# The per-layer input gets a tile of its own, and its load moves up the load queue

## The chip, the cores and the metric

The kernel runs on one core of a Trainium2 chip. The metric is device time in microseconds (us) of one execution; lower is better. A core has five engines that run their own instruction streams in order and wait for one another through semaphores: TensorE (PE: matrix products, weight loads beside them), VectorE (DVE), ScalarE (ACT), GpSimd (POOL) and SyncE (SP), which here issues nearly all loads from memory.

## The reference

One layer of a decoder trunk on 256 tokens of width 1024, in float32. Three token mixers run in parallel: sparse attention with an indexer that keeps the top 64 keys, dilated attention in which three groups of queries share keys and values, and block attention. Each adds a relative-position bias to its logits. Their gated sum goes through an output product and a layer norm, then through a feed-forward part and a second layer norm. The per-layer input p enters only near the end:

```
proj = x @ w_in                                  # queries, keys, values of the three mixers
gates = sigmoid(x @ w_gate)
merged = gates[0]*(o_a @ w_br_a) + gates[1]*(o_b @ w_br_b) + gates[2]*(o_c @ w_br_c)
x = layer_norm(ALPHA*x + merged @ w_out, ln1_g, ln1_b)
h = square(relu(x @ w_up)) @ w_down
ple = sigmoid(x @ w_ple_gate) * (p[i] @ w_ple)   # p: the per-layer input, 256 tokens x 256
x = layer_norm(ALPHA*x + h + ple, ln2_g, ln2_b)
```

## The kernel before

All products run as three products of "split" operands: a float32 tile becomes a high part, rounded to the format of the products (ScalarE's cast), and a low part, the difference (VectorE's subtraction, for some weights shared with GpSimd). A weight goes through such a split on the way in: SyncE loads 512 KB or less into one of five `raw` buffers (L71), ScalarE casts it to `whi` (L75), VectorE and GpSimd write `wlo` (L79), TensorE multiplies (L136). A load can go out once the split of an earlier weight has freed its buffer.

The order on each engine is set by the program's scheduler, from the order of the code and the data each instruction needs; `issue_after(ins)` adds the rule that what is written inside stands behind `ins` on that engine.

The stretch that matters lies between the dilated attention and the block attention:

- The dilated attention treats two pairs of heads, j = 0 and 1. For each, `toeplitz` loads two bias tiles T (three loads each, from a table in memory, L188), `slots` computes the logits and the softmax in two large buffers with the tag `eb` (pool `wk2`, two buffers), and `attend` transposes the result (L314), casts and splits it into `pt` (L321, L322), multiplies it with the values V (L324, L325) and drains the product: ScalarE copies one half to `ov` (L328), VectorE adds the halves twice (L329 to `ov`, L330 to `o`). `pair_out` splits `o` into `op` (L333, L334).
- Then the per-layer input, transposed on the host, is loaded into `pr` (L471), cast to `ph` (L472) and split to `pl` (L473). `ph` and `pl` are kept; they are multiplied only after the first layer norm. The tile `pr` takes one of the two `eb` buffers.
- Then the values of the block attention are computed (weights `wvb`), and for j = 0, 1, 2 a key tile (`k_pair`, L228 and L229), a query tile (`q_pair`, L217 and L218) and their logits (`logits`, L274). In between stand products for the gates, `fill("g")`, whose result ScalarE turns into G (L241).

```
pr = wk2.tile([128, 2, S], F32, name="pr", tag="eb")     # L470
nc.sync.dma_start(pr, pT)
act.copy(ph, pr)
dve.tensor_tensor(pl, pr, ph.bitcast(F32), op=ALU.subtract)
values(u_vb, 384, 5, 6, False)
```

Of the kernel before, what the change touches and what calls it, by code (L numbers as in the profile page):

```python
# [11 lines left out]
F32 = mybir.dt.float32  # L12
F32R = mybir.dt.float32r
ALU = mybir.AluOpType
# [6 lines left out]
S = 256  # L21
# [10 lines left out]
N_U = 384  # L32
# [63 lines left out]
def hybrid_layer(ctx: ExitStack, tc: tile.TileContext, x0, xn, pT, wqk, wva, wvb, wg, wbc, wba,  # L96
                 wout, wup, wdq, wdn, wpg, wple, lnrow, rel, mask, out):
    nc = tc.nc
    pe, act, dve, pool = nc.tensor, nc.scalar, nc.vector, nc.gpsimd
# [22 lines left out]
    ph = keep.tile([128, 2, S], F32R, name="ph")  # L122
    pl = keep.tile([128, 2, S], F32R, name="pl")
# [5 lines left out]
    t = banks.tile([128, 512], F32, name="b4", tag="b4")  # L129
# [23 lines left out]
    pm = mid.enter_context(tc.tile_pool(name="pm", bufs=1))  # L153
# [9 lines left out]
    def add(*a):  # L163
        i = n_u[0]
        n_u[0] += 1
        return W.add(*a, by=DV if i < 58 else "v")
# [6 lines left out]
    for t in TASKS:  # L173
# [8 lines left out]
        else:  # L182
            u_q.append([add(wqk[int(t) - FIRST], 1024)])

    def toeplitz(h0, step):
        t = tp.tile([128, 3, 256], F32, name="T", tag="T")
        for i in range(3):
            nc.sync.dma_start(t[:, i], bass.AP(  # L188
                tensor=tabd.tensor,
                offset=tabd.offset + (h0 + i * step) * COPIES * N_U + 127,  # L190
                ap=[[N_U - 16, 8], [N_U - 1, 16], [1, 256]]))
        return t


# [39 lines left out]
    def fill(what):  # L234


        for w in what:
            if w == "g":
                ps = mmbank(256)
                gemm(ps, u_g[n_g[0]], xs)  # L240
                act.activation(G[:, n_g[0]], ps, AF.Tanh, scale=0.5)  # L241
                n_g[0] += 1
                continue
            f = n_c[0]
            n_c[0] += 1
            hi, lo = W.get(u_bc[f][0])
            ps = mmbank(512).rearrange("p (i s) -> p i s", i=2)
            for i, (k0, k1) in enumerate(((3, 5), (5, 8))):
                for k in range(k0, k1):
                    c = slice((k - 3) * 128, (k - 2) * 128)  # L250
                    prod(ps[:, i], (hi[:, c], lo[:, c]), (op[:, k, 0], op[:, k, 1]), k == k0,
                         k == k1 - 1)
            g = G[:, 3 * f + 1:3 * f + 3]
            dve.scalar_tensor_tensor(g, g, 1.0, ps, op0=ALU.add, op1=ALU.mult)
            dve.tensor_tensor(g[:, 0], g[:, 0], g[:, 1], op=ALU.add)
# [26 lines left out]
    op = pm.tile([128, 8, 2, S], F32R, name="op")  # L282

    def values(units, n, h0, heads, withiw):
        pss = [mmbank(512) for _ in range(2)]
        for i in range(4):
            hi, lo = W.get(units[i])
            for j in range(2):
                k = 2 * i + j
                c = slice(j * n, (j + 1) * n)  # L290
                for b in range(2):
                    t = slice(b * 128, (b + 1) * 128)
                    prod(pss[b][:, :n], (xh[:, k, t], xl[:, k, t]), (hi[:, c], lo[:, c]),
                         k == 0, k == KT - 1)
        v_out(pss, n, h0, heads, withiw)
# [7 lines left out]
            dve.tensor_tensor(V[:, b, h0:h0 + heads, DH:128], src,  # L303
                              V[:, b, h0:h0 + heads, 0:DH].bitcast(F32), op=ALU.subtract)

    n_pt = [0]

    def attend(heads, o):

        ts = []  # L310
        for i, (P, vh, h) in enumerate(heads):
            t = next(ps_t)
            for c in (1, 2, 0):
                m = pe.transpose(t[:, 128 * c:128 * c + 128], P[:, 128 * c:128 * c + 128], ident)  # L314
                if i or c != 1:
                    tc.keep_in_program_order(m)
            ts.append(t)
        for t, (P, vh, h) in zip(ts, heads):
            pt = pts[n_pt[0] % 2]
            n_pt[0] += 1  # L320
            act.copy(pt[:, 0], t[:, 0:384])  # L321
            dve.tensor_tensor(pt[:, 1], t[:, 0:384], pt[:, 0].bitcast(F32), op=ALU.subtract)  # L322
            v = next(ps_t).rearrange("p (a s) -> p a s", a=2)
            pe.matmul(v, lhsT=V[:, 0, vh], rhs=pt[:, :, 0:256], start=True, stop=False)  # L324
            pe.matmul(v[:, :, 128:256], lhsT=V[:, 1, vh], rhs=pt[:, :, 256:384], start=False,  # L325
                      stop=True)
            x = wk2.tile([64, 2, S], F32, name="ov", tag="ov")
            act.copy(x, v[64:128])  # L328
            dve.tensor_tensor(x, v[0:64], x, op=ALU.add)  # L329
            dve.tensor_tensor(o[64 * h:64 * h + 64], x[:, 0], x[:, 1], op=ALU.add)  # L330
# [26 lines left out]
    def slots(qs, k, Ts, vh, o):  # L357

        es = [wk2.tile([128, 3, 384], F32, name="eb", tag="eb") for _ in range(2)]
        mxs = [sm.tile([128, 2, 3], F32, name="mxb", tag="mxb") for _ in range(2)]  # L360
        for g in range(3):
            s = logits(qs[g], k)
            for h in range(2):
                for b, t in enumerate((Ts[h][:, g, 128:256], Ts[h][:, g, :])):
                    dve.tensor_tensor_reduce(es[h][:, g, QC[b]], s[h][:, QC[b]], t, op0=ALU.add,
                                             op1=ALU.min, scale=1.0, scalar=-GONE,
                                             accum_out=mxs[h][:, b, g:g + 1])
        for h in range(2):
            e = es[h]
            m = sm.tile([128, 2], F32, name="mx", tag="mx")  # L370
            den = sm.tile([128, 2], F32, name="den", tag="den")
            dve.tensor_reduce(m, mxs[h], axis=AX.X, op=ALU.min)
            for b in range(2):
                act.activation(e[:, :, QC[b]], e[:, :, QC[b]], AF.Exp, bias=m[:, b:b + 1],
                               scale=-1.0, accum_out=den[:, b:b + 1])
            pool.tensor_tensor(e[:, 0], e[:, 0], e[:, 1], op=ALU.add)
            added[0] = pool.tensor_tensor(e[:, 0], e[:, 0], e[:, 2], op=ALU.add).ins
            scale_rows(e[:, 0], den)
        attend([(es[h][:, 0], vh + h, h) for h in (1, 0)], o)
# [36 lines left out]
    tp, wk, wk2, sm = (right(n, b) for n, b in (("tp", 3), ("wk", 3), ("wk2", 2), ("sm", 6)))  # L416
# [39 lines left out]
    for j in range(2):  # L456
        ps = feat(5 + 4 * j)
        k = k_pair(ps)
        fill("g")
        qs = []  # L460
        for g in range(3):
            qs.append(q_pair(feat(6 + 4 * j + g)))
            if g:
                fill("g")
        o = opair()
        Ts = [toeplitz(6 + 2 * j + h, 4) for h in range(2)]
        slots(qs, k, Ts, 1 + 2 * j, o)
        pair_out(o, 3 + j)
        fill("g")
    pr = wk2.tile([128, 2, S], F32, name="pr", tag="eb")  # L470
    nc.sync.dma_start(pr, pT)  # L471
    act.copy(ph, pr)  # L472
    dve.tensor_tensor(pl, pr, ph.bitcast(F32), op=ALU.subtract)  # L473
    values(u_vb, 384, 5, 6, False)
    fill("g")
    for j in range(3):
        ps = feat(13 + 2 * j)
        k = k_pair(ps)
        q = q_pair(feat(14 + 2 * j))
        s = logits(q, k)  # L480
        o = opair()
        for h in range(2):
            n = 2 * j + h
            if n % 3 == 0:
                T = toeplitz(18 + n, 1)
            e = head(s, T[:, n % 3, 128:256], T[:, n % 3], h)
            heads = [(e, 5 + n, h)] + (heads if h else [])
            if h:
                attend(heads, o)
            fill("g")  # L490
        pair_out(o, 5 + j)
# [4 lines left out]
    for j in range(3):  # L496
        q = q_pair(feat(19 + j))
        s = logits(q, kA)
        o = opair()
        for h in range(2):  # L500
            n = 2 * j + h
            if n % 3 == 0:
                T = toeplitz(n, 1)
            ta = wk.tile([128, 384], F32, name="ta", tag="ta")
            with tc.issue_after(W.pool):
                pool.tensor_tensor(ta[:, 0:128], T[:, n % 3, 128:256], am[:, 0:128], op=ALU.add)
                pool.tensor_tensor(ta[:, 128:384], T[:, n % 3], am[:, 128:384], op=ALU.add)
            e = head(s, ta[:, 0:128], ta[:, 128:384], h)
            heads = [(e, 0, h)] + (heads if h else [])
            if h:  # L510
                attend(heads, o)
            fill("gg" if n == 0 else "gc")
        done = pair_out(o, j)
# [153 lines left out]
    for b in range(2):  # L667
        t = slice(b * 128, (b + 1) * 128)
# [133 lines left out]
    for x in order:  # L802
# [4 lines left out]
        else:  # L807
            i = x - NP + 2
# [167 lines left out]
```

## Time and profile before

| | |
|---|---|
| median of 3 runs | 438.52 us (438.4 to 439.96) |
| the profiled execution | 436.83 us, of which the span is 435.0 us |
| TensorE busy | 424.3 us, 98% of the span |
| VectorE, ScalarE, GpSimd busy | 355.3, 274.7, 107.5 us |
| granted TensorE clock, mean | 0.996 |
| the chain that ended last | TensorE 92%, DMA 2%, VectorE 2%, ScalarE 1% |

The span runs from the first to the last instruction in the trace; the execution's own time is 1.83 us longer. A row of a timeline reads: start, length, engine, line of the kernel, operation, what is written from what, shape, count, and in brackets the idle time of the engine just before it with what ended that. A row of waits reads: who waited for whom, us in total, times, longest. Products are pipelined, so the lengths of neighbouring TensorE rows overlap; their starts tell the pace.

### The profile page before, as it was taken

What the parts mean: (1) busy time and instruction counts of PE and PEld (TensorE: products, weight loads), DVE (VectorE), ACT (ScalarE), POOL (GpSimd) and SP (SyncE); (2) the same over time, 40 slices, a digit from 0 to 9 for tenths busy, and PEclk for the clock granted to TensorE, in tenths of its full rate; (3) what the DMA queues carried; (4) which work ended last, traced back from release to release, by engine and by line L of the source; (5) the groups of instructions that cost most, each with busy time, mean ns of one, the idle gap of its engine ahead of it and who ended that gap; (6) DMA issues with size and microseconds to landing.
All of it is one profiled execution on the core that took longest, in us unless ns stands there. A gap on an engine that the chain in (4) does not pass through costs nothing.

```text
span 435.0 us, 7673 instructions
## 1 busy us (share of the span) xinstructions
PE 424.3 (98%) x2799; PEld 385.1 (89%) x2799; DVE 355.3 (82%) x625; ACT 274.7 (63%) x490; POOL 107.5 (25%) x98
## 2 busy tenths in 40 slices
PE   8999999999999999999999999999999999999993
PEld 8999999998999999999887888888888888888882
DVE  4978977577666588869988779999988898998984
ACT  6775375585777777746625567778887855665500
POOL 2564355392634656700000000000100000000001
PEclk9999999999999999999999999999999999999998
DMA  8897765465555334474980865656895378758411
GB/s 290 300 330 226 237 182 184 157 201 192 185 166 169 128 112 152 145 199 161 358 335 0 313 219 190 190 182 196 270 281 187 104 202 280 196 195 282 149 42 57
DMA packets 27690, 86.39 MB, mean 199 GB/s; under 512 B 2884, under 2 KB 6892, under 8 KB 27268
## 3 DMA queue, kind: packets, MB, share of 16 engines
q1 hardware_dynamic: 25872, 79.54, 55.5%
q0 software_dynamic: 640, 2.17, 2.8%
q10 hardware_dynamic: 1140, 4.19, 2.7%
q8 instruction: 22, 0.36, 0.3%
q14 instruction: 16, 0.13, 0.1%
HBM read 83.99 MB, written 1.90 MB: 197 GB/s over the span
## 4 chain that ended last, share of the span: by engine, by line
PE 92%; DMA 2%; issue 2%; DVE 2%; ACT 1%; POOLq 0%; POOL 0%; SPq 0%; DVEq 0%
PE mm L136 40%; PE b L136 23%; PE mm L705 14%; PE mm L707 7%; PE b L274 3%; PE b L413 2%; DMA G<-in_x_dram 1%; PE b L314 1%; DMA pr<-in_pT_dram 1%; PE b L324 1%; PE b L325 0%; DVE o L330 0%; DVE ov L329 0%; POOLq L972 0%; POOL rs L630 0%
## 5 line engine op out<-in xcount | busy, mean ns | idle before, releaser
L79 DVE TENSOR_TENSOR wlo<-raw,whi 128x1024 fp32r<-128x1024 f32 (+5 forms) x146 | 158.4, 1096 | 37.3 <-ACT whi L75 32.7
L75 ACT CAST whi<-raw 128x1024 fp32r<-128x1024 f32 (+3 forms) x146 | 146.1, 1011 | 46.6 <-PE b L136 11.7
L79 POOL TENSOR_TENSOR wlo<-raw,whi 128x384 fp32r<-128x384 f32 (+3 forms) x58 | 79.0, 1369 | 81.4 <-ACT whi L75 72.3
L136 PE MATMUL mm<-xl,whi 128*128 128x256 f32 x336 | 95.6, 284 | 0.0
L136 PE MATMUL mm<-xh,whi 128*128 128x256 f32 x336 | 95.0, 283 | 0.0
L136 PE MATMUL mm<-xh,wlo 128*128 128x256 f32 x336 | 94.7, 282 | 0.0
L136 PEld LDWEIGHTS mm<-xl,whi 128*128 128x128 f32 x336 | 63.3, 188 | 1.5
L705 PE MATMUL mm<-x,whi 128*128 128x512 f32 x256 | 64.1, 392 | 0.0
L136 PEld LDWEIGHTS mm<-xh,whi 128*128 128x128 f32 x336 | 63.3, 188 | 0.6
L136 PEld LDWEIGHTS mm<-xh,wlo 128*128 128x128 f32 x336 | 63.3, 188 | 0.3
L705 PEld LDWEIGHTS mm<-x,whi 128*128 128x128 f32 x256 | 46.1, 189 | 8.3
L136 PE MATMUL b<-whi,hT 128*128 128x512 f32 (+2 forms) x164 | 51.8, 381 | 0.0
L707 PEld LDWEIGHTS mm<-x,wlo 128*128 128x128 f32 x256 | 34.9, 190 | 2.5
L753 POOL DMA_DIRECT2D rows<-in_wdq_dram x4 | 3.6, 908 | 135.0 <-DVE wlo L79 81.7
L707 PE MATMUL mm<-x,wlo 128*128 128x256 f32 x256 | 35.7, 282 | 0.0
L136 PEld LDWEIGHTS b<-whi,hT 128*128 128x128 f32 x164 | 30.5, 188 | 5.8
L136 PE MATMUL b<-wlo,hT 128*128 128x512 f32 (+2 forms) x82 | 31.2, 381 | 0.0
L630 POOL TENSOR_TENSOR rs<-rs,half 128x1 f32<-128x1 f32 x4 | 4.1, 1032 | 101.5 <-DVE rs L629 101.5
L710 DVE TENSOR_REDUCE r<-mm 128x256 f32<-128x512 f32 x32 | 22.0, 688 | 5.2 <-PE mm L707 5.2
L241 ACT ACTIVATE G<-mm 128x256 f32<-128x256 f32 x24 | 9.1, 381 | 23.0 <-PE mm L136 22.9
L136 PE MATMUL mm<-op,whi 128*128 128x256 f32 x128 | 23.6, 281 | 0.0
L136 PE MATMUL b<-whi,x 128*128 128x512 f32 x64 | 20.4, 395 | 0.3 <-ACT x L658 0.3
(162 smaller groups left out, 736.6 us busy)
## 6 DMA issues: line engine op xcount, KB each, us to landing
raw<-in_wup_dram SPq DMA_DIRECT2D x32, 512.0 KB
raw<-in_wg_dram SPq DMA_DIRECT2D x24, 512.0 KB
raw<-in_wqk_dram SPq DMA_DIRECT2D x18, 512.0 KB
raw<-in_wdn_dram SPq DMA_DIRECT2D x16, 512.0 KB
raw<-in_wdq_dram SPq DMA_DIRECT2D x12, 512.0 KB
raw<-in_wout_dram SPq DMA_DIRECT2D x8, 512.0 KB
raw<-in_wpg_dram SPq DMA_DIRECT2D x8, 512.0 KB
T<-tabd SPq DMA_DIRECT2D x24, 128.0 KB
```

Of the source, the lines that this page charges most:

```text
L75: nc.scalar.copy(hi, r)
L79: low = e.tensor_tensor(lo[:, c], r[:, c], hi[:, c].bitcast(F32), op=ALU.subtract)
L136: m = pe.matmul(ps, lhsT=a[x], rhs=b[y], start=first and i == 0, stop=last and i == 2)
L241: act.activation(G[:, n_g[0]], ps, AF.Tanh, scale=0.5)
L274: m = pe.matmul(ss[h][:, QC[b]], lhsT=q[d, x, c], rhs=k[d, y, 0:128 * (b + 1)], start=i == 0, stop=i == 2)
L314: m = pe.transpose(t[:, 128 * c:128 * c + 128], P[:, 128 * c:128 * c + 128], ident)
L324: pe.matmul(v, lhsT=V[:, 0, vh], rhs=pt[:, :, 0:256], start=True, stop=False)
L413: pe.matmul(first[f], lhsT=w[:, k, 128 * f:128 * f + 128], rhs=x[:, k], start=k == i == 0, stop=k == KT - 1 and i == 2)
L630: pool.tensor_tensor(rs, rs, half, op=ALU.pow)
L705: pe.matmul(ps, lhsT=hi[:, cs[k]], rhs=x1[:, :, k], start=k == 0, stop=False)
L707: pe.matmul(ps[:, :, 0], lhsT=lo[:, cs[k]], rhs=x1[:, :, k, 0], start=False, stop=k == KT - 1)
L710: dve.tensor_reduce(r, ps.rearrange("p b a t -> p b t a"), axis=AX.X, op=ALU.add)
```

## The change

`pr` becomes a tile of 2 KB per partition in the pool `pm`, which holds what lives through the first half of the kernel. Its load stands behind the last load that `toeplitz` issued up to then, which is the third load of the second pair's second bias tile. Cast and split stand behind the last `pt` cast and the last `pt` split of the second pair.

```
     def toeplitz(h0, step):
         t = tp.tile([128, 3, 256], F32, name="T", tag="T")
         for i in range(3):
-            nc.sync.dma_start(t[:, i], bass.AP(
+            table[0] = nc.sync.dma_start(t[:, i], bass.AP(
...
-                ap=[[N_U - 16, 8], [N_U - 1, 16], [1, 256]]))
+                ap=[[N_U - 16, 8], [N_U - 1, 16], [1, 256]])).ins
...
-            act.copy(pt[:, 0], t[:, 0:384])
-            dve.tensor_tensor(pt[:, 1], t[:, 0:384], pt[:, 0].bitcast(F32), op=ALU.subtract)
+            cast[0] = act.copy(pt[:, 0], t[:, 0:384]).ins
+            cast[1] = dve.tensor_tensor(pt[:, 1], t[:, 0:384], pt[:, 0].bitcast(F32),
+                                        op=ALU.subtract).ins
...
-    pr = wk2.tile([128, 2, S], F32, name="pr", tag="eb")
-    nc.sync.dma_start(pr, pT)
-    act.copy(ph, pr)
-    dve.tensor_tensor(pl, pr, ph.bitcast(F32), op=ALU.subtract)
+    pr = pm.tile([128, 2, S], F32, name="pr")
+    with tc.issue_after(table[0]):
+        nc.sync.dma_start(pr, pT)
+    with tc.issue_after(cast[0]), tc.issue_after(cast[1]):
+        act.copy(ph, pr)
+        dve.tensor_tensor(pl, pr, ph.bitcast(F32), op=ALU.subtract)
```

What this makes of the order on the engines. On SyncE, at the loads of the second pair's last bias tile (T_1228), of the block attention's first bias tile (T_1578) and of the weights of its values (`wvb`), there stood before:

```order
L71 DMA raw_1117<-in_wvb_dram 128x768
L188 DMA T_1228<-tabd_377 128x1x256 x3
L188 DMA T_1578<-tabd_377 128x1x256 x2
L71 DMA raw_1150<-in_wvb_dram 128x768
L188 DMA T_1578<-tabd_377 128x1x256
```

and now stands:

```order
L71 DMA raw_1117<-in_wvb_dram 128x768
L190 DMA T_1228<-tabd_377 128x1x256 x3
L475 DMA pr_1373<-in_pT_dram 128x512
L190 DMA T_1578<-tabd_377 128x1x256
L71 DMA raw_1150<-in_wvb_dram 128x768
L190 DMA T_1578<-tabd_377 128x1x256 x2
```

The load of pr has come up to here from a place 16 rows further down, between two weight loads, and one load of T_1578 has gone behind the second `wvb` load.

On ScalarE, from the last `pt` cast of the second pair to the drain of its product, before:

```order
L321 CAST pt1_117<-b3_1316 128x384
L241 ACTIVATE G_114<-mm_1459 128x256
L75 CAST whi_1495<-raw_1493 128x1024
L472 CAST ph_82<-pr_1373 128x512
L328 COPY ov_1325<-b2_1322 64x512
```

and now:

```order
L323 CAST pt1_117<-b3_1316 128x384
L477 CAST ph_82<-pr_1373 128x512
L243 ACTIVATE G_114<-mm_1459 128x256
L75 CAST whi_1495<-raw_1493 128x1024
L331 COPY ov_1325<-b2_1322 64x512
```

The cast of pr has moved ahead of one G and one weight cast.

On VectorE, from the last `pt` split of the second pair to the sums in `o`, before:

```order
L322 TENSOR_TENSOR pt1_117<-b3_1316,pt1_117 128x384
L79 TENSOR_TENSOR wlo_1496<-raw_1493,whi_1495 128x640
L473 TENSOR_TENSOR pl_83<-pr_1373,ph_82 128x512
L329 TENSOR_TENSOR ov_1325<-b2_1322,ov_1325 64x512
L329 TENSOR_TENSOR ov_1334<-b3_1331,ov_1334 64x512
L229 TENSOR_TENSOR k_1525<-mm_1492,k_1525 128x256
L330 TENSOR_TENSOR o_1223<-ov_1325 64x256
L330 TENSOR_TENSOR o_1223<-ov_1334 64x256
```

and now:

```order
L324 TENSOR_TENSOR pt1_117<-b3_1316,pt1_117 128x384
L478 TENSOR_TENSOR pl_83<-pr_1373,ph_82 128x512
L79 TENSOR_TENSOR wlo_1496<-raw_1493,whi_1495 128x640
L332 TENSOR_TENSOR ov_1325<-b2_1322,ov_1325 64x512
L332 TENSOR_TENSOR ov_1334<-b3_1331,ov_1334 64x512
L333 TENSOR_TENSOR o_1223<-ov_1325 64x256
L231 TENSOR_TENSOR k_1525<-mm_1492,k_1525 128x256
L333 TENSOR_TENSOR o_1223<-ov_1334 64x256
```

The split of pr has moved ahead of one weight split, and the key split (k_1525) behind the first sum in `o`. On TensorE the twelve products of the first block logits (L274) go one product ahead. GpSimd's order is unchanged.

More of the change, by code (lines that the diff above doesn't have):

```diff
@@ L183, in hybrid_layer @@
             u_q.append([add(wqk[int(t) - FIRST], 1024)])
+    table = [None]
     def toeplitz(h0, step):
@@ L304, in v_out @@
                               V[:, b, h0:h0 + heads, 0:DH].bitcast(F32), op=ALU.subtract)
-    n_pt = [0]
+    n_pt, cast = [0], [None, None]
     def attend(heads, o):
```

## The prediction

> **What bounds the kernel now.** I read the page first, then who waited for whom on TensorE, then the chain that ended last, then the timelines of the engines around the one place where that chain leaves TensorE. From the page:
>
> ```profile
> span 435.0 us, 7673 instructions
> PE 424.3 (98%) x2799; PEld 385.1 (89%) x2799; DVE 355.3 (82%) x625; ACT 274.7 (63%) x490; POOL 107.5 (25%) x98
> ```
>
> TensorE is busy for 98% of the span; only a stall of TensorE can give time back. Its waits in the whole span, from the list of waits:
>
> ```profile
> PE b L131 <- POOL ident masks.py:199: 1.7, 1, 1.7
> PE b L274 <- DVE q L218: 1.1, 1, 1.1
> PE b L136 <- ACT x L658: 0.3, 1, 0.3
> ```
>
> After the start there are two stalls, and the larger is a product of L274 (queries times keys) that waits for VectorE to split a query. The chain that ended last shows what stands behind it (start, length, what):
>
> ```profile
> 96.54 5.08 DMA pr<-in_pT_dram
> 101.64 0.63 ACT ph L472
> 102.30 0.69 DVE pl L473
> 102.99 1.20 DVE ov L329 x2
> 104.19 0.34 DVE k L229
> 104.55 0.43 DVE o L330
> 105.00 1.12 DVE o L330
> 106.13 0.74 DVE wlo L79
> 107.13 0.42 DVE q L218
> ```
>
> The load of pr takes 5.08 us; its two splits stand in the in-order streams of ScalarE and VectorE, so everything behind them there waits for it: the drain of the attention output (L329, L330), the key split (L229), the query split (L218). The size of the stall, from TensorE's timeline:
>
> ```profile
> 106.12 0.28 PE L136 MATMUL mm<-xh,wlo 128*128 128x256 f32 x1
> 106.23 0.28 PE L136 MATMUL mm<-xl,whi 128*128 128x256 f32 x1
> 107.59 0.96 PE L274 MATMUL b<-k,q 64*128 64x128 f32 x12 [1.08 <-DVE q L218]
> ```
>
> Products there start 0.11 to 0.12 us apart, so L274 could have started at 106.23 + 0.12 = 106.35, and started at 107.59: the stall costs **1.24 us** (the idle column says 1.08, because it counts from the end of the last pipelined product).
>
> **The change, part by part.** *ScalarE.* Its rows around the cast of pr:
>
> ```profile
> 95.37 0.86 ACT L321 CAST pt<-b 128x384 fp32r<-128x384 f32 x2
> 96.62 0.38 ACT L241 ACTIVATE G<-mm 128x256 f32<-128x256 f32 x1 [0.38 <-PE mm L136]
> 96.90 1.05 ACT L75 CAST whi<-raw 128x1024 fp32r<-128x1024 f32 x1
> 101.64 0.62 ACT L472 CAST ph<-pr 128x512 fp32r<-128x512 f32 x1 [3.70 <-DMA pr<-in_pT_dram]
> 102.29 1.07 ACT L328 COPY ov<-b 64x512 f32<-64x512 f32 x2
> 103.39 0.38 ACT L228 CAST k<-mm 128x256 fp32r<-128x256 f32 x1
> 106.16 0.41 ACT L333 CAST op<-o 128x256 fp32r<-128x256 f32 x1 [1.45 <-DVE o L330]
> 106.47 0.38 ACT L217 ACTIVATE q<-mm 128x256 fp32r<-128x256 f32 x1
> ```
>
> The cast of pr (0.62) now follows the pt casts. It starts near 96.2 and ends near 96.8, filling the 0.38 of idle time ahead of L241; L241 slips by about 0.1 and the weight cast behind it ends near 98.1. The 3.70 of idle time goes.
>
> *VectorE and GpSimd.*
>
> ```profile
> 98.61 1.17 DVE L79 TENSOR_TENSOR wlo<-raw,whi 128x640 fp32r<-128x640 f32 x1
> 102.30 0.69 DVE L473 TENSOR_TENSOR pl<-pr,ph 128x512 fp32r<-128x512 f32 x1 [2.52 <-ACT ph L472]
> 106.06 0.81 DVE L79 TENSOR_TENSOR wlo<-raw,whi 128x640 fp32r<-128x640 f32 x1
> ```
>
> ```profile
> 98.08 1.01 POOL L79 TENSOR_TENSOR wlo<-raw,whi 128x384 fp32r<-128x384 f32 x1 [1.01 <-ACT whi L75]
> 104.79 1.07 POOL L79 TENSOR_TENSOR wlo<-raw,whi 128x384 fp32r<-128x384 f32 x1 [5.70 <-ACT whi L75]
> ```
>
> VectorE's split of pr (0.69) now stands between the pt splits and the weight split. The weight split took 1.17 beside GpSimd's row at 98.08 and 0.81 with GpSimd idle, so whatever stands at 98.61 pays about 0.36 more: pl runs 98.61 to about 99.65, the weight split to about 100.5.
>
> *What is late next.* The drain needs the products with V:
>
> ```profile
> 99.26 0.39 PE L324 MATMUL b<-pt,V 128*128 128x512 f32 x1
> 99.49 0.28 PE L325 MATMUL b<-pt,V 128*128 128x256 f32 x1
> 99.85 0.28 PE L136 MATMUL mm<-xl,whi 128*128 128x256 f32 x1
> ```
>
> They end at 99.77 and the key's products at 100.13. ScalarE then copies both ov (1.07), the key (0.38) and casts a weight (1.05): at most 99.2 + 2.5, near 101.8. VectorE does ov twice (1.20) to 101.7, the first o (0.43) to 102.15, the key (0.34, now behind the first o) to 102.5. GpSimd's share of that weight (1.07) runs into the second o, which took 1.12 beside such a row and 0.43 alone: I take the dear one, to 103.6. ScalarE's cast of o and query (0.41 + 0.38) ends near 104.4; VectorE's weight split (0.81), its split of o and then of the query (0.42 for the query, the same taken for o, which has the same shape) end near 105.3. TensorE comes to L274 at 106.23 (it now stands one product earlier). The query is 0.9 us early even so, and the key 3.7. I therefore book the whole 1.24 as gain and no new wait.
>
> [...]
>
> *SyncE.* The load leaves its old place and goes behind the last bias tile of the dilated pairs:
>
> ```profile
> 58.09 3.23 SPq L188 DMA_DIRECT2D T<-tabd  x5
> 61.43 0.39 SPq L71 DMA_DIRECT2D raw<-in_wvb_dram  x1
> 96.54 0.38 SPq L471 DMA_DIRECT2D pr<-in_pT_dram  x1
> 97.82 2.36 SPq L71 DMA_DIRECT2D raw<-in_wqk_dram  x2
> ```
>
> Three bias loads of 0.65 bring it to about 60.0, and it needs 0.38. One bias load now stands ahead of the next weight load where two stood, so that load goes out at about 61.05 instead of 61.43; two bias loads come after it, for a tile first read past 107 us (by the softmax behind L274). At the old place the next load was issued 0.9 after pr's issue ended, so it was not pr that held it: nothing is gained there. The loads that pr is moved past start 0.38 later at most. Landing: 5.08 us was measured while the DMA was nearly full; at the new place it is about half busy:
>
> ```profile
> 54.00:66.00 12.00, 12.00 (x107) 11.73 (x106) 9.00 (x37) 8.48 (x17) 6.93 (x7) 1.00 0.57 173
> 96.50:102.00 5.50, 5.50 (x47) 5.41 (x46) 3.27 (x4) 1.68 (x3) 1.58 (x2) 1.00 0.95 334
> ```
>
> (the last two columns are the DMA's busy share and GB/s). Even at 5.08 it has landed by 65.1, 31 us before its first reader. What it can hold up is the weight load behind it, whose cast is this:
>
> ```profile
> 73.69 0.82 ACT L75 CAST whi<-raw 128x768 fp32r<-128x768 f32 x1
> ```
>
> That is 12.6 us after its issue; 5.08 for a loaded landing plus 256 KB at 173 GB/s (1.5 us) leaves 6 us. Cost taken: nothing; if that cover failed, at most the 1.5. The 2 KB tile itself removes pr's wait for the old buffer, which the transposes of the second pair gave free; no instruction is added. From below, a gain beyond 1.24 needs another stall, and only the 0.3 of L136 is left.
>
> **Sum.** −1.24 + 0. The profiled execution took 436.83 us (span 435.0 and 1.83 around it), so 435.6 by its own clock; the median of the runs, 438.52, lies 1.69 above it, and I carry the difference over: **437.3 us**. TensorE waits for nothing else but 0.3 us behind 107.59, so the gain should reach the end.
>
> **The rivals.**
> *A, GpSimd takes the slack.* The query is early by 0.9. Beyond the collisions booked, the first o could pay another 0.69 and the second weight split 0.36: 1.05, just over the slack, and L274 would wait 0.1 to 0.6. It decides from a query split that ends past 106.2. Time 437.4 to 437.9. [...]
> *B, nothing comes of it.* Another wait of the same length stands behind pr's. For it: ScalarE's cast of o waited 1.45 for VectorE in any case. Against it: that wait was itself behind pl in VectorE's stream. Time 438.5.
> *C, slower.* The 256 KB ahead of the value weights delay the load behind them, and TensorE stands still in the value products. It needs a delay over 6 us where I find 1.5; once past that point a loaded landing (5.08) less the gain would give 442.4, a smaller one 439 to 441. Little speaks for it.
> *D, more.* With 256 KB less in the full stretch from 96.5 to 102 and VectorE ahead, the 0.3 at L136 goes as well: 437.0. Below that no row offers anything; only that the profiled execution itself lies 1.69 under the median shows that executions reach lower, so the case is given 436.2 to 437.0.
>
> **How the numbers follow.** Forecast 0.70, A 0.13, B 0.06, C 0.04, D 0.07. About 0.5% (2.2 us) is what a measurement of this kernel can tell from no change; 1.24 is 0.28%. Faster by more than that (below 436.3): part of D and the scatter of the runs (438.4 to 439.96), 0.05. Slower (above 440.7): most of C, 0.03. The rest, 0.92, is within. The range goes from 436.5 (most of D) to 438.6 (all of A and B); it leaves out C and the low end of D, some 0.08, and the rest of the 2 in 10 is scatter.
>
> **What would show it.** In the profile after: no wait of ScalarE for pr; the load of pr issued near 60; VectorE's query split ending between 104.5 and 106; L274 starting near 106.2 with no idle time before it; the list of TensorE's waits without L274; a span of 433.8. A pl row near 1.0 instead of 0.69 shows the collision with GpSimd. I am wrong if L274 still waits with another releaser, if TensorE waits for a weight between 66 and 96, or if the stall goes and a later one of the same size appears.

## The result and the profile after

| | before | after |
|---|---|---|
| median | 438.38 us (437.87 to 442.55, 10 runs) | 436.14 us (435.49 to 437.26, 10 runs) |
| the profiled execution | 436.83 us, span 435.0 | 436.15 us, span 434.4 |

The ratio is 0.9942, with a 95% interval of 0.9917 to 0.9968: 2.2 us faster, with the interval from 1.4 to 3.6. The forecast was 437.3 us and its range began at 436.5: the direction was right, the size not. A second sample of both kernels, further down, gave 0.9956 (0.9937 to 0.9976). (Executions over 1.5% above the fastest are left out of the counts below.)

In the profiled pair nearly everything is as forecast (the span is 434.4 us and not 433.8). The list of TensorE's waits has lost L274 (line numbers have moved by two to five: L274 is L276 now, L136 kept its number):

```profile
PE b L131 <- POOL ident masks.py:199: 1.7, 1, 1.7
PE b L136 <- ACT x L663: 0.3, 1, 0.3
```

In the chain that ended last, the rows of DMA, ScalarE and VectorE between 96.54 and 107.55 are gone; it stays on TensorE (the view ends at 112):

```profile
100.05 6.62 PE mm L136 x56
106.67 0.88 PE b L276 x12
107.55 4.57 PE mm L136 x37
```

TensorE's timeline shows the twelve logits products behind their neighbour without an idle column:

```profile
106.39 0.27 PE L136 MATMUL mm<-xh,wlo 128*128 128x256 f32 x1
106.59 0.95 PE L276 MATMUL b<-k,q 64*128 64x128 f32 x12
```

The load goes out at 60.73, and the cast of pr on ScalarE waits for nothing:

```profile
60.73 0.45 SPq L475 DMA_DIRECT2D pr<-in_pT_dram  x1
95.64 0.87 ACT L323 CAST pt<-b 128x384 fp32r<-128x384 f32 x2
96.39 0.65 ACT L477 CAST ph<-pr 128x512 fp32r<-128x512 f32 x1
96.91 0.42 ACT L243 ACTIVATE G<-mm 128x256 f32<-128x256 f32 x1
```

VectorE, from the split of pr to the split of the query (GpSimd's neighbouring row below it):

```profile
98.02 0.68 DVE L478 TENSOR_TENSOR pl<-pr,ph 128x512 fp32r<-128x512 f32 x1
98.62 1.63 DVE L79 TENSOR_TENSOR wlo<-raw,whi 128x640 fp32r<-128x640 f32 x1
102.27 1.11 DVE L333 TENSOR_TENSOR o<-ov 64x256 f32<-64x256 f32 x1
104.38 0.41 DVE L220 SCALAR_TENSOR_TENSOR q<-mm,q 128x256 fp32r<-128x256 f32 x1
```

```profile
98.39 1.19 POOL L79 TENSOR_TENSOR wlo<-raw,whi 128x384 fp32r<-128x384 f32 x1 [0.33 <-ACT whi L75]
```

The query is split at 104.79, and TensorE could take L276 at 106.39 + 0.12 = 106.51: 1.7 us of slack.

The same instructions of both traces, set side by side, differ by +0.27 us up to 96 (the loads at the start came later: ScalarE waited 3.1 us for them, and 2.7 before), by −0.89 from 115 to 222, and by −0.65 at the end. So the change took out 0.27 + 0.89 = 1.16 us where the forecast had 1.24, and 0.24 was lost again at the first layer norm, where the wait differs from one execution to the next (a second profile of the changed kernel, further down, has 1.4 us more there). The profiled pair differs by 0.7 us, the medians by 2.2. What has to be explained is the other microsecond: the profiled execution before lies 1.6 us below its median, and the one after lies on its own.

### The profile page after: what moved, and what is told of

Its sections match the earlier page's. It is cut to its first block, busy times and chain, and to the rows that moved or that the text cites. A ratio compares the mean times of both kernels' runs of the same rounds, so it can differ in the third digit from the quotient of the medians.

```text
span 434.4 us, 7671 instructions
## 1 busy us (share of the span) xinstructions
PE 424.7 (98%) x2799; PEld 385.5 (89%) x2799; DVE 355.9 (82%) x625; ACT 274.7 (63%) x490; POOL 106.7 (25%) x98
## 4 chain that ended last, share of the span: by engine, by line
PE 94%; issue 2%; DMA 2%; DVE 1%; ACT 0%; SPq 0%; POOLq 0%; POOL 0%; DVEq 0%
PE mm L136 42%; PE b L136 23%; PE mm L710 14%; PE mm L712 7%; PE b L276 3%; PE b L416 2%; DMA G<-in_x_dram 2%; PE b L316 1%; PE b L327 1%; PE b L328 0%; SPq L404 0%; POOLq L977 0%; PE b L661 0%; POOL rs L635 0%; DVE Y L642 0%
## 5 line engine op out<-in xcount | busy, mean ns | idle before, releaser
L79 POOL TENSOR_TENSOR wlo<-raw,whi 128x384 fp32r<-128x384 f32 (+3 forms) x58 | 78.1, 1353 | 81.4 <-ACT whi L75 77.1
L136 PE MATMUL mm<-xl,whi 128*128 128x256 f32 x336 | 95.7, 285 | 0.0
L136 PE MATMUL mm<-xh,whi 128*128 128x256 f32 x336 | 94.9, 283 | 0.0
L136 PE MATMUL mm<-xh,wlo 128*128 128x256 f32 x336 | 94.7, 282 | 0.0
L136 PEld LDWEIGHTS mm<-xl,whi 128*128 128x128 f32 x336 | 63.3, 188 | 1.7
L136 PEld LDWEIGHTS mm<-xh,whi 128*128 128x128 f32 x336 | 63.3, 188 | 0.4
L136 PEld LDWEIGHTS mm<-xh,wlo 128*128 128x128 f32 x336 | 63.3, 188 | 0.3
L136 PE MATMUL b<-whi,hT 128*128 128x512 f32 (+2 forms) x164 | 51.8, 381 | 0.0
L136 PEld LDWEIGHTS b<-whi,hT 128*128 128x128 f32 x164 | 30.5, 188 | 5.8
L136 PE MATMUL b<-wlo,hT 128*128 128x512 f32 (+2 forms) x82 | 31.2, 381 | 0.0
L136 PE MATMUL mm<-op,whi 128*128 128x256 f32 x128 | 23.6, 281 | 0.0
L136 PE MATMUL b<-whi,x 128*128 128x512 f32 x64 | 20.4, 395 | 0.3 <-ACT x L663 0.3
```

The costliest lines, as they stand in the source:

```text
L79: low = e.tensor_tensor(lo[:, c], r[:, c], hi[:, c].bitcast(F32), op=ALU.subtract)
L136: m = pe.matmul(ps, lhsT=a[x], rhs=b[y], start=first and i == 0, stop=last and i == 2)
```

## The experiments

The first four experiments ask whether the wait for pr is the whole of it: the kernel before once more, and three edits. Theory W says that it is, and that the profiled execution merely had a short wait; theory P that 1.24 us come from the wait and some 1.0 from something else.

**The kernel before again** (no edit).

> The kernel before, unchanged. Measured so far: medians 438.38 before and 436.14 after, 2.24 apart, where the stall seen in the one profile of before was 1.24. Theory W (the wait is all of it): the profiled execution of before was a short one (436.83, under the lowest of 10 timed ones, 437.87), because pr landed early in it; in this profile pr lands later than 5.1 us after its issue and L274 starts about 2.2 us late (1.8 to 3). Theory P (the wait is 1.24, and the remaining 1.0 comes from another place): L274 again about 1.2 late, landing about 5.1, the extra time elsewhere. Both: ratio 1.000 to before.

Measured: 437.94 us (436.72 to 441.58), ratio 1.0002 (0.9979 to 1.0026). Nothing but scatter lies between two copies. In its profiled execution (436.92 us) pr lands 5.06 us after its issue and L274 starts 1.19 us late. That is what P expected of this trace; W had expected a start some 2.2 us late.

**The early load alone.** Tile and load as in the change; cast and split go back to where they stood.

```
     with tc.issue_after(table[0]):
         nc.sync.dma_start(pr, pT)
-    with tc.issue_after(cast[0]), tc.issue_after(cast[1]):
-        act.copy(ph, pr)
-        dve.tensor_tensor(pl, pr, ph.bitcast(F32), op=ALU.subtract)
...
+        if j == 0:      # behind the cast and the split of the next weight
+            with tc.issue_after(W.cast[u]), tc.issue_after(W.sub[u]):
+                act.copy(ph, pr)
+                dve.tensor_tensor(pl, pr, ph.bitcast(F32), op=ALU.subtract)
```

> The changed kernel, with the load early in its own tile, but cast and split of pr at their old place (behind the next weight cast and weight split). W: nothing waits for pr, so the whole gain: about 436.1 (ratio 0.995). A theory in which the new place of the splits matters gives less: 1.0 or more of the gain missing, 437.1 and up.

Measured: 436.54 us (435.76 to 440.45), ratio 0.9958 (0.9935 to 0.9981). No wait at the logits; where the two splits stand does not matter.

**A tile of 2 KB more** in the kernel before.

```
+    pm.tile([128, 2, S], F32, name="spare")
     pr = wk2.tile([128, 2, S], F32, name="pr", tag="eb")
```

> The kernel before with an unused tile of 2 KB per partition in the pool pm, at the address that pr has in the changed kernel; all instructions in the order of before. W: as before, 438.4 (ratio 1.000). P, if the remaining 1.0 came from the new addresses: 437.4 (0.9977).

Measured: 438.26 us (436.42 to 441.32), ratio 0.9997 (0.9971 to 1.0022). It tells little of the layout: no instruction of the trace touches the spare tile, and whether it moves any address is not shown, so I count this run as another copy of the kernel before. That the place of the tile is not the gain, the next run shows instead. Its profile is of use, though; its execution took 438.38 us and has two stalls:

```profile
PE b L274 <- DVE q L218: 1.5, 1, 1.5
PE b L657 <- DVE Y L638: 1.0, 1, 1.0
```

**The late load kept, the splits later.** The tile stays in the `eb` buffer and the load at its old place; only the cast and the split go behind those of the first query.

```
     nc.sync.dma_start(pr, pT)
-    act.copy(ph, pr)
-    dve.tensor_tensor(pl, pr, ph.bitcast(F32), op=ALU.subtract)
...
+        if j == 0:
+            with tc.issue_after(last[0]), tc.issue_after(low[0]):
+                act.copy(ph, pr)
+                dve.tensor_tensor(pl, pr, ph.bitcast(F32), op=ALU.subtract)
```

> The kernel before with the load of pr where it was, in the old buffer, but its cast and split behind the first query's cast and split. W: nothing that TensorE needs stands behind pr, so the whole gain: about 436.1 (ratio 0.995), with L274 at its pace and pr still landing at about 101.6 or later. P, if the remaining 1.0 comes from taking 256 KB out of the full stretch from 96.5 to 102: only the 1.24, so about 437.1 (0.997).

Measured: 436.42 us (436.18 to 436.98), ratio 0.995 (0.993 to 0.997). The load goes out at 97.34, as late as ever, nobody waits for it, and the logits start without an idle column:

```profile
97.34 0.38 SPq L471 DMA_DIRECT2D pr<-in_pT_dram  x1
```

```profile
104.25 0.38 ACT L217 ACTIVATE q<-mm 128x256 fp32r<-128x256 f32 x1
104.53 0.61 ACT L480 CAST ph<-pr 128x512 fp32r<-128x512 f32 x1
```

```profile
107.13 0.95 PE L274 MATMUL b<-k,q 64*128 64x128 f32 x12
```

So neither the load's place nor the tile's brings the gain. What brings all of it is that the cast and the split no longer stand, waiting, ahead of the attention's drain in two in-order streams. P has lost its "something else". W still had to say why 1.24 us in the trace are 2 us at the median. Two candidates: the wait varies (V), or a stall at this place breeds others (S).

**A stall that depends on no load.** The early-load kernel with the order of every engine written out, and the cast of pr made seven times.

```
+                again = [act.copy(ph, pr).ins for _ in range(6)]
                 act.copy(ph, pr)
```

> The kernel with the early load and the splits at the old place (which ran at 436.54 us, against 438.27 before), with the order on every engine written out so that nothing else moves, and the cast of pr made seven times in a row instead of once. Six more casts of 0.62 us hold ScalarE up to about 102.6 us, as the load did before, but by work of ScalarE alone: L274 gets a stall of 1.0 to 1.5 us that depends on no transfer. Theory V (the wait before varies: in a usual execution the load lands later than in the profiled ones): the time is tight, as after the change, and lies one constant stall above it, 437.3 to 437.9 us, with the quarter points less than 1 us apart. Theory S (a stall at this place, whatever makes it, moves TensorE against the later loads and breeds further waits): the time is as before, 438.0 to 438.6 us, and spreads as before, from 436.5 to 441 with the quarter points 2 us apart.

Measured: 438.47 us (437.67 to 440.73; quarter points 437.80 and 439.04), ratio 0.9999 (0.9979 to 1.0018). Its stall:

```profile
106.52 0.27 PE L250 MATMUL mm<-xh,wlo 128*128 128x256 f32 x1
108.06 0.95 PE L390 MATMUL b<-k,q 64*128 64x128 f32 x12 [1.27 <-DVE q L334]
```

that is 108.06 − 106.64 = 1.42 us. The changed kernel, run beside it (further down), took 436.72, so the stall costs about 1.75. The median is above V's range and in S's, the spread is nearer to V's (1.2 us between the quarter points, where the kernel before, run beside it, has 1.9; and nothing below 437.67, where that one reaches 437.00). By itself this did not decide.

**Twelve casts.**

> The same with twelve casts instead of seven: ScalarE is held up for some 3 us more, to about 105.5 us, and the stall of L274 becomes 4 to 4.5 us. Theory V: constant again, about 3 us above the run with seven casts (440.2 to 440.9), tight. Theory S: over 441 us, and wide.

Measured: ratio 1.0082 (1.0053 to 1.0112); the median is 442.36 us (441.54 to 443.75) over five executions, 442.57 with a sixth that the count leaves out. That is above what V expected and where S put it, but the list of waits shows no later wait that this kernel has and the one with seven casts has not. TensorE is idle in two pieces before the logits, 3.6 us together:

```profile
105.52 0.28 PE L250 MATMUL mm<-xl,whi 128*128 128x256 f32 x1
108.52 0.58 PE L250 MATMUL mm<-xh,whi 128*128 128x256 f32 x1 [2.72 <-DVE k L345]
110.88 1.65 PE L390 MATMUL b<-k,q 64*128 64x128 f32 x12 [0.93 <-DVE q L334]
```

That is 2.3 us more idle time than with seven casts, while the time grew by 3.9. The rest stands in the granted clock, the share of its full clock that TensorE was given, which no theory so far had named (stretch, PE busy, granted clock, DMA share, GB/s):

```profile
107.00:108.00 1.00, 0.00 (x0) 0.98 0.00 0
108.00:109.00 1.00, 0.48 (x2) 0.50 0.00 0
...
113.00:114.00 1.00, 1.00 (x7) 0.50 0.26 66
114.00:115.00 1.00, 1.00 (x7) 0.60 0.68 229
115.00:116.00 1.00, 1.00 (x11) 1.00 0.87 320
```

TensorE comes out of the stall at half its clock, from about 107.96 (0.98 is 0.04 us at a half) to 114.80: 6.8 us. The mean granted clock of these executions is 0.987 to 0.990, against 0.993 to 0.996 with seven casts in all but one.

**The changed kernel again** (no edit).

> The changed kernel once more, as a second sample of its spread beside the two above. Both theories: 436.1 us (435.8 to 436.5), ratio to before 0.993 to 0.997. A median above 437 would say that the gain of 2.2 us was partly the luck of the first sample.

Measured: 436.72 us (435.82 to 437.94), ratio 0.9956 (0.9937 to 0.9976). The median lies 0.2 above the expected range, the ratio within it. Both samples together: 436.49 over 22 executions, all with a mean clock of 0.993 or more. The profiled execution took 437.92 us, 1.2 above the median of its sample, with no wait at the logits. What it has is a wait at the first layer norm:

```profile
PE b L661 <- DVE Y L642: 1.4, 1, 1.4
```

The profile of the early load alone (438.00 us, 1.5 above its median) has the same 1.4 us there. So a profiled execution can lie over 1 us off its median for reasons other than the wait for pr.

**The kernel before, one more profile.**

> The kernel before, unchanged, for one more profile of it. Theory V: its stall at L274 and the landing of pr vary from execution to execution (so far 1.24, about 1.2 and 1.65 us with landings of 5.1, 5.1 and 5.5), and an execution above 438.3 us has a stall above 2 us there. Theory S: the stall stays at 1.2 to 1.7 us, and what makes an execution long stands later in the trace, as it did in the one of 438.38 us (1.0 us at the first layer norm).

This execution took 441.31 us, and it has both things at once. The load lands late, the stall is long:

```profile
97.49 0.38 SPq L471 DMA_DIRECT2D pr<-in_pT_dram  x1
```

```profile
103.73 0.62 ACT L472 CAST ph<-pr 128x512 fp32r<-128x512 f32 x1 [4.86 <-DMA pr<-in_pT_dram]
```

```profile
107.36 0.28 PE L136 MATMUL mm<-xl,whi 128*128 128x256 f32 x1
109.67 0.96 PE L274 MATMUL b<-k,q 64*128 64x128 f32 x12 [2.03 <-DVE q L218]
```

and behind it the clock falls to a half:

```profile
110.00:111.00 1.00, 1.00 (x13) 1.00 0.75 147
111.00:112.00 1.00, 1.00 (x9) 0.72 0.91 365
112.00:113.00 1.00, 1.00 (x6) 0.50 0.41 53
113.00:114.00 1.00, 1.00 (x6) 0.50 0.66 270
114.00:115.00 1.00, 1.00 (x7) 0.57 0.87 250
115.00:116.00 1.00, 1.00 (x11) 1.00 0.66 221
```

A stall of 109.67 − 107.48 = 2.19 us, and then 0.28 + 0.50 + 0.50 + 0.43 = 1.71 us of clock that was not granted, which is half of 3.4 us, from about 111.44 to 114.86. In the profile that the prediction was made from the clock is 1.00 throughout this stretch. Two other waits, 0.8 us at the first products (L413) and 0.7 at the first layer norm (L656), add to this execution's length. The next runs put the clock to the test: theory C (a long stall takes the clock with it) against N (the clock has no part).

**Twelve casts, and TensorE kept busy.** 40 products that nothing reads, in the logits' own bank, fill the stall.

```
+            for n in range(26 + 14):
+                m = pe.matmul(ss[1][:, 0:256], lhsT=xh[:, 0, 0:128], rhs=xh[:, 0], start=True,
+                              stop=True)
```

> The kernel with twelve casts (442.57 us; TensorE idle for 2.7 and 0.9 us there, and the granted clock at one half from 108.0 to about 114.6 us), and 40 products more that nothing reads, written into the logits' own bank before the logits: 26 ahead of the five products that stand before L274, 14 right ahead of L274. TensorE is kept busy through the stall, the casts and all waits of the other engines stay. Theory C (the second half of what a long stall costs is the granted clock, which falls to one half behind idle time of TensorE): the clock stays at 1.00, mean 0.993 or more, L274 still starts near 110.9, and the time falls to half of the 3.7 us from 110.9 to 114.6 less, 440.7 us (440.2 to 441.2). Theory N (the clock has no part in it, or falls for another reason): 442.3 us or more, mean clock 0.987 to 0.990.

Measured: 441.10 us (440.42 to 441.95); mean clock 0.994 to 0.996 in all six. The logits of the profiled execution start 1.3 us later than without the fillers. Of that, 1.1 us was there ahead of the stall (the last product before it starts at 106.61 here and at 105.52 there, since this execution waited 1.0 us at the first products), and 0.2 is the fillers'. The kernel is 1.3 us faster all the same:

```profile
106.61 0.28 PE L250 MATMUL mm<-xl,whi 128*128 128x256 f32 x1
110.43 1.83 PE L388 MATMUL b<-xh 128*128 128x256 f32 x14
112.19 0.95 PE L398 MATMUL b<-k,q 64*128 64x128 f32 x12
```

```profile
111.00:112.00 1.00, 1.00 (x11) 1.00 0.00 0
112.00:113.00 1.00, 1.00 (x15) 1.00 0.64 86
113.00:114.00 1.00, 1.00 (x12) 1.00 0.88 340
```

From the start of the logits on, the two profiled executions need 442.36 − 110.88 = 331.5 and 441.29 − 112.19 = 329.1 us: 2.4 us less with the clock kept up. C holds, with the median at the upper end of its range and the logits at 112.19 where it expected them near 110.9.

**Nine casts.**

> Nine casts, between seven (438.47 us, idle time 1.27 before L274, the clock low in 1 of 12 executions) and twelve (442.57, low in all). Idle time about 2.5 us. Theory C: the clock falls in some executions and not in others, so there are two groups, about 439.7 us at a mean clock of 0.993 or more and 441 to 442 at 0.992 or less. Theory N: one group at about 440.0 us, midway between the two kernels, whatever the clock.

Measured: 441.67 us (439.77 to 442.30), ratio 1.0071 (1.0043 to 1.0099), and two groups, as C says: 439.77 and 439.87 us at a mean clock of 0.994; 441.59, 441.75, 441.98 and 442.30 at 0.987 to 0.989. One program, with a stall that hangs on no load, keeps its clock or loses it, and that is worth 2.0 us. The profiled execution was one of the first two; it had idle times of 0.76 and 1.51 us in this stretch and a clock of 1.00.

**No load at all**, for the price of the early load.

```
-    pr = pm.tile([128, 2, S], F32, name="pr")
-    with tc.issue_after(table[0]):
-        nc.sync.dma_start(pr, pT)
+    pr = xh[:, 0:2].bitcast(F32)
```

> The changed kernel without the load of pr at all: cast and split read the first two tiles of the high part of x instead, so the per-layer product has another input (that part of the result is left out). It tells what the early load of 256 KB costs among the value weights. If it is free, as the prediction has it: 436.1 to 436.7 us, as the changed kernel. If the load delays a weight: faster than the changed kernel by up to its 1.5 us of transfer, near 435.2.

Measured: 436.65 us (435.55 to 437.69), ratio 0.9965 (0.9949 to 0.9981): as the changed kernel (436.14 and 436.72). The early load shows no cost.

**The kernel before, a fifth profile.**

> The kernel before, unchanged, for a fifth profile. Theory C: a time up to 439 us goes with a stall of 1.2 to 1.7 us at L274 and a granted clock of 1.00 behind it; a time of 439.5 us or more goes with idle time near 2 us there, or elsewhere, and a clock of one half for about 3 us behind it, as in the execution of 441.31 us. Theory N: a long execution with the clock at 1.00 throughout the middle of the trace.

437.79 us, idle for 0.67 us before L274, clock 1.00 behind it. C has the clock right; the stall, 0.83 us, is shorter than the 1.2 to 1.7 that it named. The five profiled executions of the kernel before, from the rows of SyncE, ScalarE and TensorE (landing: from the issue of pr's load to the start of its cast; stall: from 0.12 us behind the start of the last product to L274; other waits: TensorE's at the first products, L413, and at the first layer norm, L656, where the list has them):

| time | load issued | cast starts | landing | stall | clock behind it | other waits |
|---|---|---|---|---|---|---|
| 437.79 | 97.29 | 101.99 | 4.70 | 0.83 | 1.00 | 0.6, 0.4 |
| 436.92 | 96.92 | 101.98 | 5.06 | 1.19 | 1.00 | none |
| 436.83 | 96.54 | 101.64 | 5.10 | 1.24 | 1.00 | none |
| 438.38 | 96.51 | 102.04 | 5.53 | 1.65 | 1.00 | 0.2, 1.0 |
| 441.31 | 97.49 | 103.73 | 6.24 | 2.19 | 0.50 for 3.4 us | 0.8, 0.7 |

The stall is the landing less 3.87 us in the first four rows, to 0.02; in the last it is 0.18 shorter than that. V is right in kind: the wait varies, by 1.4 us over five executions, and a later landing lengthens the stall one for one or nearly so. On top come the clock, in the last row, and the other waits, which is why the shortest stall does not go with the shortest time.

## Why the prediction was off

*The mechanism, right.* Two splits that waited for a late load held the drain, the key and the query back in two in-order streams. The run that kept the late load and moved only the splits shows it (436.42 us, ratio 0.995), and no wait took the place of the one removed.

*The term 1.24, right for an execution that keeps its clock.* Of 91 executions of the kernel before among the experiments (counting the copies), 67 have a mean clock of 0.993 or more, and their median is 437.81 us. Of 40 executions without the wait (both samples of the change, the early load, the late splits), 39 have, and their median is 436.54. The difference is 1.27.

*The step that failed: the carrying over of 1.69 us.* "The profiled execution took 436.83 us ..., the median ... lies 1.69 above it, and I carry the difference over", and before that "a gain beyond 1.24 needs another stall". That took one draw of the stall for its usual cost, and the gap for something outside the change. Part of the gap went with the stall, through the clock that a long one takes away: 24 of the 91 executions are at 0.992 or less, with a median of 440.17 us, against 1 of 40 without the wait. Of the 22 executions from 439.5 us up, 20 are among the 24. They pull the median of all 91 to 438.23; against 436.54 that is 1.7 us, which is the size of the gain that I would give now: some 0.45 more than 1.24, without another stall.

*The rest of the miss is luck.* The forecast lay 1.14 us above the measured 436.14. The failed step accounts for those 0.45 us. Another 0.29 is the sample of three that the prediction started from (438.52 against 438.23), and 0.40 the first sample of the changed kernel (436.14 against 436.54); the second, 436.72, lies 0.6 above the first and within the forecast's range. With two samples of one kernel that far apart, these parts are rough. And most of the gap that was carried over did belong outside the change: 436.54 is still 0.95 above 436.83 − 1.24, and the waits at the first products and the first layer norm are such things.

Only one of those 24 was profiled: that it is this stall which takes the clock in the others is inferred from that one, from the casts, and from their absence without the wait.

*Case D* came nearest (436.2 to 437.0), for its last half sentence: executions reach lower than the median. Its reason, the 0.3 at L136, was wrong; that wait is still there, 0.3 long.

*The slack.* Forecast 0.9 us, found 1.7. The weight split behind pl was booked at 0.81 and took 1.63, and pl took 0.68 and not 1.04; but the drain's other rows came earlier than their bounds. In the trace the weight split beside GpSimd's row at 98.39 took 1.63 us and the one at 103.31, with GpSimd idle, 0.81; what makes it longer there, no run shows. Neither of the collisions that rival A had named came (the first o took 0.42, the second weight split 0.81); the one that did, behind pl, fell within the slack.

*The load.* Forecast to go out at about 60.0 and to cost nothing: issued at 60.73, and the kernel without any load is no faster (436.65 us).

*The clock.* It was absent from the prediction: the rows that it showed said 1.00. The fall has a depth and a length in the rows: 0.50, for 3.4 us in the execution of 441.31 us (products start 0.21 to 0.22 us apart there, 0.11 to 0.12 at 1.00) and for 6.8 us in the profiled one with twelve casts. How idle TensorE has to be for it is not shown. In the execution of 441.31 us it had been idle for 2.03 us and was busy again for 1.8 us (109.67 to 111.44) when the clock fell; the program with nine casts, idle for 0.76 + 1.51 us in its profiled execution, kept its clock in that and one other and lost it in four. What puts that one program on either side, no run here shows.

## What to carry to other kernels

Before a stall is costed, ask what it depends on: the one here, which ends with a transfer, was 0.83 to 2.19 us long over five executions of one program, so a profile gives one draw of it, and the distance between the profiled execution and the median may in part be that same stall. Look at the clock of every execution as well as at the profile's: here, with TensorE busy for 97% of the span, a stall of 2.19 us was followed by 1.71 us of clock that was not granted, and with nine casts the clock was worth 2.0 us. Work that waits for a load and is needed only much later belongs behind what is needed now in an in-order stream, even if the load itself stays late (here, moving the two splits alone gave the ratio 0.995).

## What the hardware showed beyond that

The fall of the clock can come behind the stall, not in it: idle from 107.64 to 109.67, full clock to about 111.4, half of it to about 114.9, while TensorE was busy again. The kernel with twelve casts was made faster by useless products: 40 of them took 1.3 us off it (442.36 to 441.10). And a landing of the same 256 KB at the same place in the program varied from 4.70 to 6.24 us over five executions.
